# The attention's value products on one core: feature-major float32 for all query blocks, two kv heads in the two halves of a bank

## The chip, the cores and the metric

The kernel runs on one core of a Trainium2 chip. The metric is the device time of one execution in microseconds (us). The engines that matter here are TensorE (PE in the profile; its weight loads stand apart as PEld), VectorE (DVE), ScalarE (ACT), GpSimd (POOL) and SyncE (SP, which issues most DMAs). They run side by side, each through its own instructions in order, and wait for one another by semaphores.

## The reference, cut to what matters

```
def dsa_mixer(x, cos, sin, w_in, w_o):          # 512 tokens, 16 heads of 64, 4 kv heads, top_k = 128
    q, k, v, iq, ik, iw = split(x @ w_in)       # q, k, iq, ik get partial rotary
    for each block of 128 queries:
        score  = sum over index heads of iw * relu(iq . ik / 8), causal
        sel    = top_k(score, 128)
        logits = q . k[sel] / 8, -inf where not causal       # each kv head serves 4 heads
        p      = softmax(logits)
        o      = p @ v[sel]
    return o @ w_o
```

The whole is four sub-layers: this attention, a squared-ReLU MLP, a gated linear attention (GLA), another MLP, each followed by a layer norm. float32 in and out.

## The kernel before, in words

Products are made in one of two ways. `float32r` operands are streamed once; where accuracy needs it an operand is split into a high and a low float32r part (`split`, `stack_q`, `stack_k`, the pairs `hi, lo`), and two or three products are summed. `float32` operands are multiplied as they are; the trace shows two TensorE records for each such matmul, one for other dtypes and for transposes.

The attention works on 16 steps, `steps[i] = (b, g)`: query block b of 128 queries (0 to 3), kv head g (0 to 3) with its four heads. Block b sees (b + 1) key blocks kb of 128 keys. Selection is a mask: `top_k` finds the 128 best scores of each row and leaves -1e30 on the others in `sc[b]`.

- `logits(i, j)` makes the scores of head j of step i into a `qk` bank (two of them), VectorE adds the mask and takes the row's extreme (`pr`, `mx`, L704), ScalarE takes the exponential in place (L708, or L710, which also sums the row into `den`).
- `turn(i, kb)` transposes the four heads' 128 x 128 probabilities into a `tps` bank (L717), and ScalarE copies them to a tile `pT` of 128 keys x 512 (four heads of 128 queries): L720 for blocks 0 and 1; L725 for blocks 2 and 3, where VectorE also takes the low part (L726).
- `values(i)`, for blocks 0 and 1 (`b < STACKED`): token-major float32. For each head and kb the probabilities are the weights and `vn[:, kb, g, :]` is streamed, 64 values and a column of ones (65 columns), into the `po` bank; the ones give the softmax's denominator (L735, 48 matmuls). VectorE divides (L747, L738).
- `values_t(i, kb)`, for blocks 2 and 3: feature-major float32r. The weights are v's high and low parts side by side (`vs`, 128 columns, made once by `split_v`), 512 columns of probabilities are streamed, high and then low (L768, L769, 28 each). `back` then copies the sum to SBUF (L774), transposes it back (L779), and adds the two halves and divides (L781, L782, L783), once for each step.
- After a block's four steps `to_xt` transposes the block's output for the output projection.

`blocks` writes the steps so that the logits of step i + 1 stand between the turns of step i. The values of blocks 2 and 3 follow their turns by `LAG`. The projections of the remaining queries (`natural`, L197 to L199) and of the output (`out_first`) are written between the steps.

The order that runs is not that of the source: a scheduler sets each engine's order as the kernel is built, and takes ready matmuls of a projection in between. The pools bound it: three `ps` banks (projections, and the feature-major sums), two `qk`, one `po`, two `tps`, eight `pT` tiles.

One other place in the kernel bears on this: in the GLA, L990 and L997 are float32 matmuls whose outputs lie in 64 or 32 of a bank's 128 partitions, for L997 in four neighbouring strips of 32, one after the other.

Of the kernel before, what the change touches and what calls it, by code (L numbers as in the profile page):

```python
# [57 lines left out]
RAW_BUFS = 4  # L58
ORDER = (1, 2, 3, 0)
WARM_UP = (4, 6)  # L60
STACKED = 2
LAG = 3

_CF = {}

# [40 lines left out]
class Trunk:  # L106
# [504 lines left out]
    def attention(self, x, xs):  # L611

        nc, tc = self.nc, self.tc
        with tc.tile_pool(name="att", bufs=1) as ap:
            qT = [self.big.tile([P, A_H, P], F32R, name="big") for _ in range(NT)]
            kT = ap.tile([P, A_KV, 2, SEQ], F32R, name="kT")
            vn = ap.tile([P, NT, A_KV, 65], F32, name="vn")
            nc.vector.memset(vn[:, :, :, 64:65], 1.0)
            sc = [None] + [ap.tile([P, (b + 1) * P], F32, name=f"sc{b}") for b in range(1, NT)]
            with tc.tile_pool(name="idx", bufs=1) as ip, tc.tile_pool(name="ir", bufs=2) as it, \  # L620
                    tc.tile_pool(name="idt", bufs=3) as self.rt:
# [67 lines left out]
            def logits(i, j):  # L689

                b, g = steps[i]
                W = (b + 1) * P
                mb = self.cbias if b == 0 else sc[b]
                if j == 0:
                    pr = pp.tile([P, 4, 512], F32, name="pr")
                    mx = self.small.tile([P, 4], F32, name="mx")
                    den = self.small.tile([P, 4], F32, name="den") if b >= STACKED else None
                    live[i] = pr, mx, den
# [3 lines left out]
                nc.tensor.matmul(ps[:, :W], qT[b][:, h, :], kT[:, g, 0, :W], start=True, stop=False)  # L702
                nc.tensor.matmul(ps[:, :W], qT[b][:, h, :], kT[:, g, 1, :W], start=False, stop=True)
                nc.vector.tensor_tensor_reduce(out=pr[:, j, :W], in0=ps[:, :W], in1=mb[:, :W],  # L704
                                               scale=-(A_D ** -0.5), scalar=3.0e38, op0=OP.add, op1=OP.min,
                                               accum_out=mx[:, j:j + 1])
                if den is None:
                    nc.scalar.activation(pr[:, j, :W], pr[:, j, :W], AF.Exp, bias=mx[:, j:j + 1], scale=-1.0)  # L708
                else:
                    nc.scalar.activation(pr[:, j, :W], pr[:, j, :W], AF.Exp, bias=mx[:, j:j + 1], scale=-1.0,  # L710
                                         accum_out=den[:, j:j + 1])

            def turn(i, kb):

                tps = self.tp.tile([P, 4, P], F32, name="tps")
                for j in range(4):
                    nc.tensor.transpose(tps[:, j, :], live[i][0][:, j, kb * P:(kb + 1) * P], self.ident)  # L717
                if steps[i][0] < STACKED:
                    pT = ptp.tile([P, 4, P], F32, name="pT")
                    nc.scalar.copy(pT, tps)  # L720
                    live[i, kb] = pT
                else:
                    ph = ptp.tile([P, 4, P], F32R, name="pT")
                    pl = ptp.tile([P, 4, P], F32R, name="pT")
                    nc.scalar.copy(ph, tps)  # L725
                    nc.vector.tensor_sub(pl, tps, ph.bitcast(F32))  # L726
                    live[i, kb] = ph, pl

            def values(i):
                b, g = steps[i]  # L730
                po = self.po.tile([P, 512], F32, name="po")
                po = po[:, :260].rearrange("p (j d) -> p j d", d=65)
                for j in range(4):
                    for kb in range(b + 1):
                        nc.tensor.matmul(po[:, j, :], live[i, kb][:, j, :], vn[:, kb, g, :],  # L735
                                         start=kb == 0, stop=kb == b)
                on, rc = normalizer(b, g, po[:, :, 64])
                nc.vector.tensor_tensor(on, po[:, :, 0:64], rc, op=OP.mult)  # L738
                if g == A_KV - 1:
                    self.to_xt(live["on"], b)  # L740

            def normalizer(b, g, den):

                if g == 0:
                    live["on"] = op_.tile([P, DM], F32, name="on")
                rc = self.small.tile([P, 4], F32, name="rc")
                nc.vector.reciprocal(rc, den)  # L747
                on = live["on"][:, g * 256:(g + 1) * 256].rearrange("p (j d) -> p j d", d=64)
                return on, rc[:, :, None].to_broadcast([P, 4, 64])

            def split_v():

                vs = self.big.tile([P, NT * A_KV, 2, 64], F32R, name="big")
                vf = vn[:, :, :, 0:64].rearrange("p t g d -> p (t g) d")
                nc.scalar.copy(vs[:, :, 0, :], vf)
                nc.vector.tensor_sub(vs[:, :, 1, :], vf, vs[:, :, 0, :].bitcast(F32))
                live["vs"] = vs

            def values_t(i, kb):
# [8 lines left out]
                nc.tensor.matmul(ps, vs, ph, start=kb == 0, stop=False)  # L768
                nc.tensor.matmul(ps, vs, pl, start=False, stop=kb == b)  # L769
                for f in live.pop("back", []):  # L770
                    f()
                if kb == b:
# [3 lines left out]
                    def back():  # L776
                        po = self.po.tile([P, 512], F32, name="po").rearrange("p (j d) -> p j d", d=P)
                        for j in range(4):
                            nc.tensor.transpose(po[:, j, :], oT[:, j, :], self.ident)  # L779
                        on, rc = normalizer(b, g, live[i][2])  # L780
                        nc.scalar.copy(on, po[:, :, 64:128])  # L781
                        nc.vector.tensor_add(on, on, po[:, :, 0:64])  # L782
                        nc.vector.tensor_tensor(on, on, rc, op=OP.mult)  # L783
                        if g == A_KV - 1:
                            self.to_xt(live["on"], b)

# [2 lines left out]
            def blocks():  # L789

                for j in range(4):
                    logits(0, j)
                turned = []
                for i, (b, g) in enumerate(steps):
                    if (b, g) == (STACKED, 0):
                        split_v()
# [12 lines left out]
                for a in turned:  # L809
                    values_t(*a)  # L810
                for f in live.pop("back"):
                    f()

# [423 lines left out]
```

## Time and profile before

| what | value |
|---|---|
| device time, median of 3 runs | 1145.86 us (1145.68 to 1147.49) |
| the profiled execution | 1145.4 us, its span 1143.6 us |
| PE busy over the span | 1126.0 us (98%) |
| DVE busy | 883.2 us (77%) |
| ACT busy | 563.7 us (49%) |
| TensorE clock granted | 0.998 |
| blocks 0 and 1, with the projections among them | about 108 to 147 us of the span |
| block 2 | about 147 to 176 us |
| block 3, with the output projections among its steps | about 176 to 216 us |

Busy time of PE is not work at its peak: matmuls are pipelined, each record contains the way through the array, and the ends are modelled. The cost of a matmul in a stream is read from the distance of two starts. In a row of the timeline that joins n records, that is (length of the row minus length of one record) / (n - 1). Rows of groups give busy time and the mean duration of one, and the idle time of the engine just ahead of them.

### The profile page before, as it was taken

The page shows a single profiled execution, that of the slowest core. Times are in us where ns is not written, and L with a number is a line of the kernel's source. Part 1 is how long each engine was busy: PE and PEld are TensorE (multiplying, and loading weights), DVE is VectorE, ACT ScalarE, POOL GpSimd, SP SyncE. Part 2 cuts the span into 40 slices and gives each one's busy share as a digit, 9 for nine tenths or more (in the row PEclk, how much of TensorE's full clock was granted, in tenths as well). Part 3 has the DMA queues.
Part 4 walks back from the last instruction along what each step waited for, and adds up shares of the span by engine and source line. Part 5 has one row for each costly group of instructions (what it writes and reads, how often), then busy time and mean ns, then how long its engine had stood idle before and what let it go on. Part 6 is the DMA issues. An engine that isn't in the chain of part 4 may idle for free. (4 is left out here: it accounts for less than half of the span.)

```text
span 1143.6 us, 16057 instructions
## 1 busy us (share of the span) xinstructions
PE 1126.0 (98%) x6039; PEld 943.5 (82%) x6039; DVE 883.2 (77%) x1592; ACT 563.7 (49%) x973; POOL 212.9 (19%) x136
## 2 busy tenths in 40 slices
PE   9999999999999999999999999999999999999997
PEld 7887888888888888888797887888988888888875
DVE  7899997687976786786885387567696876786787
ACT  6655786543544444353356476435344444343342
POOL 0000000002123213203301255110042123213221
PEclk9999999999999999999999999999999999999999
DMA  7322130521421431441432232052222421431321
GB/s 252 98 74 75 37 112 1 154 88 38 147 84 64 148 112 47 137 142 55 112 109 77 63 112 90 23 148 74 83 91 86 148 92 56 147 117 52 127 74 74
DMA packets 58198, 109.12 MB, mean 95 GB/s; under 512 B 5205, under 2 KB 10841, under 8 KB 58121
## 3 DMA queue, kind: packets, MB, share of 16 engines
q1 hardware_dynamic: 56968, 103.91, 28.7%
q0 software_dynamic: 1152, 4.19, 1.3%
q8 instruction: 47, 0.77, 0.3%
q14 instruction: 31, 0.25, 0.1%
HBM read 105.99 MB, written 2.10 MB: 95 GB/s over the span
## 5 line engine op out<-in xcount | busy, mean ns | idle before, releaser
L142 DVE TENSOR_TENSOR w_lo<-raw,w_hi 128x1024 fp32r<-128x1024 f32 (+4 forms) x220 | 288.9, 1331 | 29.1 <-ACT w_hi L141 26.7
L141 ACT CAST w_hi<-raw 128x1024 fp32r<-128x1024 f32 (+4 forms) x220 | 223.6, 1024 | 120.6 <-PE ps L199 45.8
L197 PE MATMUL ps<-XT,w_hi 128*128 128x512 f32 (+1 forms) x640 | 236.0, 369 | 0.0
L198 PE MATMUL ps<-XT,w_hi 128*128 128x512 f32 (+1 forms) x640 | 235.5, 368 | 0.0
L199 PE MATMUL ps<-XT,w_lo 128*128 128x512 f32 (+1 forms) x640 | 235.5, 368 | 0.0
L197 PE MATMUL ps<-w_hi,XT 128*128 128x512 f32 (+5 forms) x440 | 163.7, 372 | 0.8 <-ACT w_hi L141 0.8
L198 PE MATMUL ps<-w_lo,XT 128*128 128x512 f32 (+5 forms) x440 | 160.9, 366 | 0.6 <-DVE w_lo L142 0.6
L199 PE MATMUL ps<-w_hi,XT 128*128 128x512 f32 (+5 forms) x440 | 160.3, 365 | 0.0
L198 PEld LDWEIGHTS ps<-XT,w_hi 128*128 128x128 f32 x640 | 120.7, 189 | 20.2 <-issue 0.4
L197 PEld LDWEIGHTS ps<-XT,w_hi 128*128 128x128 f32 x640 | 120.6, 189 | 20.2 <-issue 0.2
L199 PEld LDWEIGHTS ps<-XT,w_lo 128*128 128x128 f32 x640 | 120.6, 188 | 20.1 <-issue 0.2
L163 POOL TENSOR_TENSOR raw<-raw 128x1024 f32<-128x1024 f32 x14 | 34.2, 2441 | 385.4 <-DVE w_lo L142 385.4
L197 PE MATMUL ps<-w_hi,form 128*128 128x512 f32 x260 | 102.2, 393 | 0.7 <-DVE big L419 0.7
L198 PE MATMUL ps<-w_lo,form 128*128 128x512 f32 x260 | 101.4, 390 | 0.0
L199 PE MATMUL ps<-w_hi,form 128*128 128x512 f32 x260 | 101.4, 390 | 0.0
L197 PEld LDWEIGHTS ps<-w_hi,XT 128*128 128x128 f32 x440 | 82.8, 188 | 12.0 <-ACT w_hi L141 1.0
L198 PEld LDWEIGHTS ps<-w_lo,XT 128*128 128x128 f32 x440 | 82.8, 188 | 11.1 <-DVE w_lo L142 1.0
L199 PEld LDWEIGHTS ps<-w_hi,XT 128*128 128x128 f32 x440 | 82.8, 188 | 10.9
L142 DVE TENSOR_TENSOR w_lo<-t,w_hi 128x1024 fp32r<-128x1024 f32 x14 | 30.3, 2164 | 72.7 <-ACT w_hi L141 72.7
L371 DVE TENSOR_TENSOR h<-h 128x512 f32<-128x512 f32 (+1 forms) x72 | 43.7, 624 | 44.2 <-ACT h L370 44.2
L370 ACT ACTIVATE h<-ps 128x512 f32<-128x512 f32 (+1 forms) x72 | 38.7, 546 | 61.5 <-PE ps L199 54.5
L141 ACT CAST w_hi<-t 128x1024 fp32r<-128x1024 f32 x14 | 14.7, 1049 | 105.3 <-POOL t L165 105.3
(248 smaller groups left out, 1950.4 us busy)
## 6 DMA issues: line engine op xcount, KB each, us to landing
raw<-in_mlp_w_up_dram SPq DMA_DIRECT2D x64, 512.0 KB, 4.4
raw<-in_mlp_w_down_dram SPq DMA_DIRECT2D x64, 512.0 KB, 4.4
raw<-in_b_w_in_dram SPq DMA_DIRECT2D x16, 512.0 KB, 4.9
raw<-in_a_w_in_dram SPq DMA_DIRECT2D x12, 512.0 KB, 4.6
big<-in_x_dram SPq DMA_DIRECT2D x8, 512.0 KB, 4.0
raw<-in_a_w_o_dram SPq DMA_DIRECT2D x8, 512.0 KB, 4.0
raw<-in_b_w_o_dram SPq DMA_DIRECT2D x8, 512.0 KB, 4.7
raw<-in_b_w_in_dram SPq DMA_DIRECT2D x8, 346.0 KB, 3.9
```

What stands on the lines that cost most here:

```text
L141: self.nc.scalar.copy(hi, src)
L142: self.nc.vector.tensor_sub(lo, src, hi.bitcast(F32))
L163: sub(t1, b12, b11)
L197: mmul(out, lhs[0], rhs[0], start=first, stop=False, skip_group_check=more)
L198: mmul(out, lhs[0], rhs[1], start=False, stop=False, skip_group_check=more)
L199: mmul(out, lhs[1], rhs[0], start=False, stop=last, skip_group_check=more)
L370: nc.scalar.activation(h, ps[:, :step], AF.Relu)
L371: nc.vector.tensor_mul(h, h, h)
```

## The change

All four blocks now go one way, feature-major in plain float32. `turn` makes one float32 `pT` tile, with no low part. `values(i, kb)` is called for odd g only and takes the steps i - 1 and i together: two float32 matmuls of 512 columns, whose weights are v of one kv head (64 columns), the first into partitions 0 to 63 of a `ps` bank, the second into 64 to 127. `back` runs once for each pair of kv heads: four transposes bring both heads home at once, one VectorE instruction divides 512 columns by `den`. The denominators come from the exponential's row sum in all blocks. The column of ones is no longer set, `split_v` and `vs` are gone, and LAG counts positions and not turned tiles. In the lines of the changed kernel the projections are L196 to L198, the logits L701 and L702, the turns L713, the values L726, the way back L737, `to_xt` L241.

```
-STACKED = 2
-LAG = 3
+LAG = 2
...
-            nc.vector.memset(vn[:, :, :, 64:65], 1.0)
...
-                if den is None:
-                    nc.scalar.activation(pr[:, j, :W], pr[:, j, :W], AF.Exp, bias=mx[:, j:j + 1], scale=-1.0)
-                else:
-                    nc.scalar.activation(..., accum_out=den[:, j:j + 1])
+                nc.scalar.activation(..., accum_out=den[:, j:j + 1])
...
-                if steps[i][0] < STACKED:
-                    pT = ptp.tile([P, 4, P], F32, name="pT")
-                    nc.scalar.copy(pT, tps)
-                    live[i, kb] = pT
-                else:
-                    ph = ptp.tile([P, 4, P], F32R, name="pT")
-                    pl = ptp.tile([P, 4, P], F32R, name="pT")
-                    nc.scalar.copy(ph, tps)
-                    nc.vector.tensor_sub(pl, tps, ph.bitcast(F32))
-                    live[i, kb] = ph, pl
+                live[i, kb] = ptp.tile([P, 4, P], F32, name="pT")
+                nc.scalar.copy(live[i, kb], tps)
...
-                ph, pl = (a.rearrange("p j q -> p (j q)") for a in live.pop((i, kb)))
-                vs = live["vs"][:, kb * A_KV + g]
-                vs = vs.rearrange("p two d -> p (two d)")
-                nc.tensor.matmul(ps, vs, ph, start=kb == 0, stop=False)
-                nc.tensor.matmul(ps, vs, pl, start=False, stop=kb == b)
+                for m in range(2):
+                    p = live.pop((i - 1 + m, kb)).rearrange("p j q -> p (j q)")
+                    nc.tensor.matmul(ps[m * 64:(m + 1) * 64, :], vn[:, kb, g - 1 + m, 0:64], p,
+                                     start=kb == 0, stop=kb == b)
...
-                        on, rc = normalizer(b, g, live[i][2])
-                        nc.scalar.copy(on, po[:, :, 64:128])
-                        nc.vector.tensor_add(on, on, po[:, :, 0:64])
-                        nc.vector.tensor_tensor(on, on, rc, op=OP.mult)
+                        rc = self.small.tile([P, 2, 4], F32, name="rc")
+                        nc.vector.reciprocal(rc, live.pop(("den", b, g // 2)))
+                        on = live["on"][:, (g - 1) * 256:(g + 1) * 256].rearrange("p (m j d) -> p j m d", m=2, d=64)
+                        nc.vector.tensor_tensor(on, po.rearrange("p j (m d) -> p j m d", m=2), ..., op=OP.mult)
...
                         if x <= b:
                             turn(i, x)
-                            if b >= STACKED:
-                                turned.append((i, x))
-                        if len(turned) > LAG:
-                            values_t(*turned.pop(0))
-                    if i > 0 and steps[i - 1][0] < STACKED:
-                        values(i - 1)
+                            if g % 2:
+                                turned.append((now, i, x))
+                        now += 1
+                        while turned and turned[0][0] < now - LAG:
+                            values(*turned.pop(0)[1:])
```

The scheduler's order of the changed program has the 40 value matmuls in 26 runs between other TensorE work: 16 runs of one matmul, 9 of two, and one of six. Blocks 0 and 1 have 8 runs of one and 2 of two; blocks 2 and 3 the rest.

TensorE, end of block 1, before: the token-major values (L735) between logits (L702, L703), turns (L717) and the transposes of `to_xt` (L242).

```order
L702 MATMUL qk<-kT,big 128x256
L703 MATMUL qk<-kT,big 128x256
L242 MATMUL tps<-cft,on 128x128 x2
L735 MATMUL po<-vn,pT 128x65 x2
L702 MATMUL qk<-kT,big 128x256
L703 MATMUL qk<-kT,big 128x256
L735 MATMUL po<-vn,pT 128x65 x6
```

The same place now:

```order
L713 MATMUL tps<-cft,pr 128x128 x2
L726 MATMUL ps<-pT,vn 64x512
L241 MATMUL tps<-cft,on 128x128 x4
L726 MATMUL ps<-pT,vn 64x512
L241 MATMUL tps<-cft,on 128x128 x4
L726 MATMUL ps<-pT,vn 64x512
L701 MATMUL qk<-kT,big 128x256
```

The two halves of a bank no longer stand next to each other here: transposes over all 128 partitions have come in between.

TensorE in block 3, before, a turn and its two value matmuls:

```order
L702 MATMUL qk<-kT,big 128x512
L703 MATMUL qk<-kT,big 128x512
L717 MATMUL tps<-cft,pr 128x128 x4
L768 MATMUL ps<-pT,big 128x512
L769 MATMUL ps<-pT,big 128x512
```

The same place now:

```order
L713 MATMUL tps<-cft,pr 128x128 x4
L726 MATMUL ps<-pT,vn 64x512 x2
L701 MATMUL qk<-kT,big 128x512
L702 MATMUL qk<-kT,big 128x512
L713 MATMUL tps<-cft,pr 128x128 x4
```

Here the two halves have stayed together, in a run of two.

TensorE at the first turns of block 0, before: matmuls of the third query projection (L197 to L199) stand between the logits.

```order
L197 MATMUL ps<-w_hi,XT 128x512
L198 MATMUL ps<-w_lo,XT 128x512
L702 MATMUL qk<-kT,big 128x128
L717 MATMUL tps<-cft,pr 128x128
L703 MATMUL qk<-kT,big 128x128
```

The same place now:

```order
L701 MATMUL qk<-kT,big 128x128
L713 MATMUL tps<-cft,pr 128x128
L702 MATMUL qk<-kT,big 128x128
L701 MATMUL qk<-kT,big 128x128
L702 MATMUL qk<-kT,big 128x128
L713 MATMUL tps<-cft,pr 128x128 x3
```

The projection's matmuls have left block 0's logits; they now begin at block 1's first logits and stand mostly behind them.

More of the change, by code (lines that the diff above doesn't have):

```diff
@@ L696, in logits @@
                     mx = self.small.tile([P, 4], F32, name="mx")
-                    den = self.small.tile([P, 4], F32, name="den") if b >= STACKED else None
-                    live[i] = pr, mx, den
+                    if g % 2 == 0:
+                        live["den", b, g // 2] = self.small.tile([P, 2, 4], F32, name="den")
+                    live[i] = pr, mx, live["den", b, g // 2][:, g % 2, :]
                 pr, mx, den = live[i]
@@ L717, in turn, with values @@
                     nc.tensor.transpose(tps[:, j, :], live[i][0][:, j, kb * P:(kb + 1) * P], self.ident)
-                if steps[i][0] < STACKED:
-                    pT = ptp.tile([P, 4, P], F32, name="pT")
-                    nc.scalar.copy(pT, tps)
-                    live[i, kb] = pT
-                else:
-                    ph = ptp.tile([P, 4, P], F32R, name="pT")
-                    pl = ptp.tile([P, 4, P], F32R, name="pT")
-                    nc.scalar.copy(ph, tps)
-                    nc.vector.tensor_sub(pl, tps, ph.bitcast(F32))
-                    live[i, kb] = ph, pl
[L729 to L759, printed above, removed]
+                live[i, kb] = ptp.tile([P, 4, P], F32, name="pT")
+                nc.scalar.copy(live[i, kb], tps)
+            def values(i, kb):
                 b, g = steps[i]
@@ L779, in back @@
                             nc.tensor.transpose(po[:, j, :], oT[:, j, :], self.ident)
-                        on, rc = normalizer(b, g, live[i][2])
-                        nc.scalar.copy(on, po[:, :, 64:128])
-                        nc.vector.tensor_add(on, on, po[:, :, 0:64])
-                        nc.vector.tensor_tensor(on, on, rc, op=OP.mult)
+                        if g == 1:
+                            live["on"] = op_.tile([P, DM], F32, name="on")
+                        rc = self.small.tile([P, 2, 4], F32, name="rc")
+                        nc.vector.reciprocal(rc, live.pop(("den", b, g // 2)))
+                        on = live["on"][:, (g - 1) * 256:(g + 1) * 256].rearrange("p (m j d) -> p j m d", m=2, d=64)
+                        nc.vector.tensor_tensor(on, po.rearrange("p j (m d) -> p j m d", m=2),
+                                                rc.rearrange("p m j -> p j m")[:, :, :, None].to_broadcast([P, 4, 2, 64]),
+                                                op=OP.mult)
                         if g == A_KV - 1:
@@ L793, in blocks @@
                 turned = []
+                now = 0
                 for i, (b, g) in enumerate(steps):
-                    if (b, g) == (STACKED, 0):
-                        split_v()
                     for x in range(4):
@@ L801, in blocks @@
                             turn(i, x)
[L802 to L807 removed]
+                            if g % 2:
[3 more added lines that the diff above has]
+                            values(*turned.pop(0)[1:])
                     yield
[L809 to L810 removed]
+                for _, i, x in turned:
+                    values(i, x)
                 for f in live.pop("back"):
```

4 lines of the change are left out of this document (2 added, 2 removed).

## The prediction

> **What bounds the kernel now.** I read the page's busy times first, then the stages of the attention by windows, then who waits there, then the groups of instructions, and last the timeline for the distance of starts. The page:
>
> ```profile
> PE 1126.0 (98%) x6039; PEld 943.5 (82%) x6039; DVE 883.2 (77%) x1592; ACT 563.7 (49%) x973; POOL 212.9 (19%) x136
> ```
>
> The windows of blocks 0 and 1, block 2, block 3 (columns: length, then busy us of each engine, the granted clock and DMA):
>
> ```profile
> 108.00:147.00 39.00, 37.99 (x265) 32.72 (x263) 36.36 (x131) 30.88 (x64) 0.00 (x0) 1.00 0.14 43
> 147.00:176.00 29.00, 28.55 (x189) 24.30 (x188) 27.56 (x79) 26.60 (x72) 0.00 (x0) 1.00 0.27 90
> 176.00:216.00 40.00, 40.00 (x220) 32.79 (x219) 25.12 (x63) 23.54 (x55) 2.27 (x4) 1.00 0.12 37
> ```
>
> TensorE has work nearly all the time, at full clock, and DMA is light. DVE is also close to full in the first window, DVE and ACT in the second; in the third TensorE stands alone. So the change is priced on TensorE, and the other engines count where they make it wait. Its waits, first in 105 to 147, then in 147 to 216:
>
> ```profile
> PEld qk L702 <- DVE mx L704: 2.3, 5, 0.8
> ...
> PEld tps L717 <- DVE pT L726: 0.8, 3, 0.3
> PEld tps L717 <- DVE XT L245: 0.6, 1, 0.6
> ...
> PEld ps L769 <- DVE pT L726: 0.2, 1, 0.2
> ```
>
> Only 1.0 us of waiting on the low part (L726) is there to win back, although that group is 19.3 us of DVE. What follows the attention is bound by TensorE as well (98%), so a difference here is carried to the end.
>
> **Prices on TensorE.** The timeline:
>
> ```profile
> 118.62 1.05 PE L735 MATMUL po<-vn,pT 128*128 128x65 f32 x8
> ...
> 645.65 0.32 PE L198 MATMUL ps<-w_lo,XT 128*128 128x346 f32 x1
> 645.81 0.32 PE L199 MATMUL ps<-w_hi,XT 128*128 128x346 f32 x1
> 646.06 0.55 PE L997 MATMUL qk<-Q,gk 128*32 128x48 f32 x32
> 646.54 0.42 PE L197 MATMUL ps<-w_hi,XT 128*128 128x346 f32 x1
> 646.80 0.32 PE L198 MATMUL ps<-w_lo,XT 128*128 128x346 f32 x1
> 646.96 0.32 PE L199 MATMUL ps<-w_hi,XT 128*128 128x346 f32 x1
> ...
> 663.79 0.31 PE L199 MATMUL ps<-w_hi,XT 128*128 128x346 f32 x1
> 664.03 0.68 PE L990 MATMUL qk<-E 128*64 128x64 f32 x8
> ...
> 700.05 0.39 PE L197 MATMUL ps<-w_hi,XT 128*128 128x512 f32 x1
> 700.28 0.39 PE L198 MATMUL ps<-w_lo,XT 128*128 128x512 f32 x1
> ...
> 716.42 1.02 PE L1051 MATMUL po<-big,AT 128*128 128x256 f32 x4
> 717.28 1.03 PE L1051 MATMUL qk<-big,AT 128*128 128x256 f32 x4
> ...
> 719.00 0.60 PE L1034 MATMUL tps<-cft,E 128*128 128x128 f32 x4
> ```
>
> And the groups (busy us, mean ns, idle before):
>
> ```profile
> L726 DVE TENSOR_TENSOR pT<-tps,pT 128x512 fp32r<-128x512 f32 x28 | 19.3, 689 | 3.7 <-ACT pT L725 2.8
> L768 PE MATMUL ps<-pT,big 128*128 128x512 f32 x28 | 12.4, 442 | 0.0
> L735 PE MATMUL po<-vn,pT 128*128 128x65 f32 x96 | 12.4, 268 | 0.0
> L769 PE MATMUL ps<-pT,big 128*128 128x512 f32 x28 | 11.9, 423 | 0.0
> L710 ACT ACTIVATION_READ_ACCUMULATOR pr<-pr,mx 128x1 f32 x32 | 6.4, 200 | 0.0
> L779 PE MATMUL po<-cft,pT 128*128 128x128 f32 x32 | 4.8, 274 | 0.0
> L774 ACT COPY pT<-ps 128x512 f32<-128x512 f32 x8 | 4.8, 600 | 0.9 <-PE ps L769 0.9
> L783 DVE TENSOR_TENSOR on<-on,rc 128x256 f32<-128x256 f32 x8 | 3.4, 423 | 0.2
> L782 DVE TENSOR_TENSOR on<-on,po 128x256 f32<-128x256 f32 x8 | 3.3, 416 | 0.2
> L738 DVE TENSOR_TENSOR on<-po,rc 128x256 f32<-128x256 f32 x8 | 3.3, 416 | 0.0
> L781 ACT COPY on<-po 128x256 f32<-128x256 f32 x8 | 3.0, 379 | 0.7 <-PE po L779 0.6
> ```
>
> - A float32r matmul of 512 columns: 700.28 - 700.05 = 0.23 us.
> - Float32, 65 columns: (1.05 - 0.27) / 7 = 0.11 a record, two records, 0.22 us.
> - Float32, 256 columns: 717.28 - 716.42 = 0.86 for four records, so 0.43 a matmul. 512 columns then take 0.86 us, 3.7 times float32r. The number of weight columns does not shorten it: L990, 64 columns of weights and 64 streamed, needs (0.68 - 0.22) / 7 = 0.066 a record, against 0.054 by columns.
> - Side by side: L997 is 16 float32 matmuls of 48 columns in four strips. One after another they would need 16 x 0.43 x 48 / 256 = 1.29 us. From first start to last start are 0.55 - 0.21 = 0.34, with the last stream 0.38: 3.4 at a time. L990's four lie in one strip and do not overlap. So neighbours in different strips overlap, and I take a pair in two halves at 0.86 for both. A pair with an instruction over all 128 partitions in between can't, since the order on the engine holds: 0.86 each.
> - Going into strips and out: from L199 at 645.81 to L198 at 646.80 are 0.99 us. The two projections around are worth 0.16 each (645.65 to 645.81, 646.80 to 646.96), the strips 0.38. That leaves 0.29 us for one excursion: late start of the first, late start of the next, whose successor is late too. Float32 as such isn't the cause: L1051 to L1034 and the projections around them follow without a gap of this size. Bounds: 0.20 if only the two late starts count (646.06 - 645.97 and 646.54 - 646.44), 0.32 with reading error.
>
> In the Trainium skill, TensorEngine Tiling (Array Packing), Key Properties, a change of the tiling mode drains TensorE, while a change of tile within a mode does not. The page has no price for it; were there no such drain, the sum below would lose its excursions and come to +0.6 us, and with the row's 0.29 it is +8.1. The trace agrees with the rule.
>
> **The sum, part by part.**
> 1. Removed: 48 x 0.22 = 10.6 (blocks 0, 1) and 56 x 0.23 = 12.9 (blocks 2, 3), 23.5 us of TensorE.
> 2. Added: 40 matmuls in 26 runs. 16 runs of one and 9 of two take 0.86 each, the one of six takes three times that: 28 x 0.86 = 24.1. Streamed whole and always paired it would be 20 x 0.86 = 17.2; the scheduler's order costs 6.9 of it.
> 3. Excursions: 26 x 0.29 = 7.5 (5.2 to 8.3).
> 4. The transposes home: 32 before (8 steps), 32 now (8 pairs), at (0.60 - 0.27) / 3 = 0.11. Nothing; 1.7 us move from blocks 2 and 3 to blocks 0 and 1.
>
> TensorE: 24.1 + 7.5 - 23.5 = +8.1. By stage: blocks 0 and 1 +2.7 (10 x 0.86 + 10 x 0.29 + 1.7 - 10.6), blocks 2 and 3 +5.5.
>
> 5. DVE in blocks 2 and 3 loses 19.3 (L726) and 3.3 (L782), and one division of 512 columns replaces two of 256. TensorE wins the 1.0 us of its waits on L726; at most the waits of that window on DVE together, about 2.
> 6. Lost cover: in block 0 the logits wait for DVE (the 2.3 us above), and the projection's nine matmuls between them (9 x 0.23 = 2.1) have moved behind. They covered waits; DVE's own work there hardly changes (two divisions less, top-k as before). Between 0 and 2.1, taken as 1.0.
> 7. ACT in blocks 0 and 1 gets 32 row sums (6.4) and four copies of a sum (2.4), and loses one copy of v (1.0): 30.9 + 7.8 = 38.7 of 39 us. On the way from exponential to turn 0.2 us more each. I cost this at nothing since TensorE's own +2.7 lengthens that window and gives ACT room to 41.7; if that cover fails it is the third rival.
> 8. The feature-major sums of blocks 0 and 1 now take `ps` banks, which the projections use. Three are there, and the projections mostly stand behind; nothing, or one wait of a stream (0.9). The removed memset and v's split (one each, under 1.3 us of DVE) are hidden by TensorE.
>
> Sum: 8.1 - 1.0 + 1.0 = +8.1 us against the profiled execution's own 1145.4 us (span 1143.6 and 1.8 around it, 0.5 below the median of the runs). Forecast 1153.5 us, 0.7% slower.
>
> **Rivals.**
> - Excursions are hidden (other side: faster). The 0.29 was seen around short streams of 48 columns; a stream of 0.86 us may give time to load the next weights and to change over. Then +0.6 remains on TensorE, and DVE's relief of up to 2.2 decides: 1143.8 us. The point from which it decides: an excursion under 0.06 us. Against it: the first late start comes before the strips stream at all (0.09 at L997; at L990 the projection ahead starts at 663.79 and lasts 0.16, so 0.08 too), and no length of theirs can hide it; 26 x 0.09 is 2.3 us. 0.07; half hidden would be 1149, in my range.
> - Halves do not overlap: only strips of 32 were seen. Then 12 pairs more at 0.86, +10.3: 1163.8 us. For it only that 64-wide neighbours don't occur in this trace. 0.07.
> - ACT sets the pace of blocks 0 and 1. The highest share the trace shows over a stage is 26.60 of 29 (92%); at that share 38.7 us need 42.1, 3.1 over the window, about what TensorE adds there anyway (2.7). If the waits of both add up and do not overlap, 8.1 + 3.1: 1156.6 us. 0.14.
> - The relief is larger: TensorE's records hide waits, and all waiting of block 2 goes (28.55 of 29 busy, yet by the prices above about 2 us of it is not streaming). Together with excursions at 0.20: 8.1 - 2.3 - 2.2 - 1.0 = +2.6, 1148.0. 0.10, half of it below the bound of what can be told.
>
> **How the numbers follow.** The main case has 0.62: 1153.5, from 1149.0 (short excursions, full relief, no lost cover) to 1159.6 (dear excursions, lost cover 2.1, a bank wait, some ACT). A measurement of this kernel tells 0.2%, 2.3 us, from no change. Faster than that: the larger part of the first rival, 0.06. Within: its rest and half of the fourth, 0.07. Slower: the rest, 0.87. The range reaches down towards the fourth rival and up over ACT's: 1147.8 to 1160.5, which leaves out the first rival and the second, and a little of the main case.
>
> **What would show it.** L726 (the new value matmuls) as 80 records of 64 weight columns, first and second half with starts a few ns apart in runs of two, 0.86 us and more apart where broken; 0.3 us between the neighbours of a run beyond its stream; no subtraction into `pT` on DVE, whose busy time falls by some 23 us; TensorE still over 95% busy from 108 us to the attention's end, which comes about 8 us later. The forecast is wrong if starts of the halves lie 0.43 us or more apart in runs of two, if the excursion is far from 0.29, or if TensorE's waits on ACT in blocks 0 and 1 grow beyond 3 us.

## The result, and the profile after

The changed kernel takes 1159.33 us (median; 1157.71 to 1160.01), the kernel before 1145.80 us beside it. The ratio is 1.0109, with a 95% interval from 1.0094 to 1.0123: 13.5 us slower. Forecast were 1153.5 us, within 1147.8 to 1160.5.

The profiled execution took 1157.71 us with a span of 1155.9, against 1143.6 before: 12.3 us. The first line of the page:

```profile
PE 1136.3 (98%) x5967; PEld 931.2 (81%) x5967; DVE 861.7 (75%) x1538; ACT 564.3 (49%) x996; POOL 212.8 (18%) x136
```

DVE has lost 21.5 us and TensorE has gained 10.3, at the same share. Where the time lies is read from marks, the starts of some instructions in both traces:

| mark | before, us | after, us | difference |
|---|---|---|---|
| first logits of block 0 (128 columns) | 108.44 | 108.31 | -0.1 |
| first logits of block 1 (256 columns) | 119.49 | 121.57 | +2.1 |
| first logits of block 2 (384 columns) | 145.01 | 150.29 | +5.3 |
| first logits of block 3 (512 columns) | 165.00 | 171.49 | +6.5 |
| first ReLU of the MLP | 252.62 | 263.31 | +10.7 |
| end | 1143.63 | 1155.94 | +12.3 |

So 5.3 us come in blocks 0 and 1, 5.4 in blocks 2 and 3 with what follows them, and 1.6 far behind the attention, where no line was changed. Windows of the changed kernel over blocks 0 and 1, over block 2, and over block 3 (length, busy us of PE, PEld, DVE, ACT, POOL, then TensorE's clock, DMA share and GB/s):

```profile
108.00:147.00 39.00, 35.76 (x189) 25.22 (x188) 35.05 (x116) 29.96 (x85) 0.00 (x0) 0.96 0.23 70
147.00:180.00 33.00, 33.00 (x176) 19.86 (x176) 17.79 (x58) 27.25 (x72) 0.00 (x0) 1.00 0.12 46
180.00:228.00 48.00, 47.87 (x238) 32.36 (x237) 16.19 (x46) 25.36 (x55) 2.28 (x4) 1.00 0.09 21
```

In the first window TensorE has fallen from 37.99 to 35.76 of 39 us, and its clock is 0.96 where it was 1.00. From 147 us on it is full as before, and DVE, nearly full in block 2 before (27.56 of 29), is at 17.79 of 33. The waits between 105 and 147 us show who holds TensorE up:

```profile
PEld qk L701 <- DVE mx L703: 2.6, 4, 1.0
...
PE qk L701 <- DVE mx L703: 2.0, 4, 0.9
PEld ps L726 <- ACT pT L715: 1.9, 4, 0.8
PEld tps L713 <- ACT pT L715: 1.3, 2, 0.8
```

The logits' matmuls themselves now wait 2.0 us for DVE, with nothing between them. Before, from 105 to 216 us, these were all the waits of matmuls that the view lists:

```profile
PE qk L702 <- DVE mx L704: 0.6, 2, 0.4
PE tps L717 <- DVE XT L245: 0.3, 1, 0.3
```

So 0.6 us of the 2.3 were waits of matmuls, and the rest was a wait of weight loads with matmuls still in the pipe. Block 0 in three windows, and the same stretch of the kernel before in two:

```profile
108.00:114.00 6.00, 3.94 (x27) 3.00 (x26) 5.97 (x26) 5.94 (x17) 0.00 (x0) 0.99 0.00 1
114.00:117.40 3.40, 3.40 (x14) 2.26 (x14) 3.28 (x15) 2.83 (x13) 0.00 (x0) 0.51 0.00 0
117.40:121.50 4.10, 3.74 (x20) 1.99 (x17) 3.06 (x14) 2.83 (x10) 0.00 (x0) 1.00 0.00 0
```

```profile
108.00:114.00 6.00, 5.22 (x35) 3.80 (x34) 5.96 (x26) 5.70 (x12) 0.00 (x0) 1.00 0.00 1
114.00:119.50 5.50, 5.42 (x42) 4.62 (x41) 5.50 (x29) 4.17 (x12) 0.00 (x0) 1.00 0.00 0
```

TensorE is busy for 3.94 of the first 6 us instead of 5.22, and then its clock stands at half speed for 3.4 us. The trace of the kernel before has half clock only at its end.

The new value matmuls, as a group and on the timeline (start, duration of the row, then the operation; each matmul is two records):

```profile
L726 PE MATMUL ps<-pT,vn 128*64 128x512 f32 x80 | 30.7, 629 | 0.7 <-ACT pT L715 0.7
```

```profile
154.55 0.45 PE L701 MATMUL qk<-kT,big 128*128 128x384 f32 x1
154.83 0.34 PE L702 MATMUL qk<-kT,big 128*128 128x384 f32 x1
155.10 1.08 PE L726 MATMUL ps<-pT,vn 128*64 128x512 f32 x4
156.11 0.88 PE L584 MATMUL tps<-ident_r,hl 128*128 128x128 f32 x8
...
160.78 1.07 PE L726 MATMUL ps<-pT,vn 128*64 128x512 f32 x2
161.79 0.55 PE L713 MATMUL tps<-cft,pr 128*128 128x128 f32 x3
...
219.24 2.79 PE L726 MATMUL ps<-pT,vn 128*64 128x512 f32 x12
221.96 0.66 PE L241 MATMUL tps<-cft,on 128*128 128x128 f32 x4
```

Two matmuls side by side (x4) take 1.01 us from their start to the next instruction's, one alone (x2) also 1.01: the halves overlap fully, their records start 6 to 7 ns apart, and a broken pair pays twice. Six matmuls take 2.72, so a stream is (2.72 - 1.01) / 2 = 0.86 us. What is over in a run of one, 0.15, with the late start of the first record (0.09) and of the instruction behind the next (0.06 to 0.11), makes 0.30 to 0.36 for an excursion (a change into strips and out again) in all runs where nothing was waited for.

### The profile page after: what moved, and what is told of

Read it like the earlier page. It is cut to its first block, busy times and chain, and to the rows that moved or that the text cites. A ratio compares the mean times of both kernels' runs of the same rounds, so it can differ in the third digit from the quotient of the medians.

```text
span 1155.9 us, 15873 instructions
## 1 busy us (share of the span) xinstructions
PE 1136.3 (98%) x5967; PEld 931.2 (81%) x5967; DVE 861.7 (75%) x1538; ACT 564.3 (49%) x996; POOL 212.8 (18%) x136
## 3 DMA queue, kind: packets, MB, share of 16 engines
q1 hardware_dynamic: 56968, 103.91, 28.4%
## 5 line engine op out<-in xcount | busy, mean ns | idle before, releaser
L196 PE MATMUL ps<-XT,w_hi 128*128 128x512 f32 (+1 forms) x640 | 236.0, 369 | 0.0
L197 PE MATMUL ps<-XT,w_hi 128*128 128x512 f32 (+1 forms) x640 | 235.5, 368 | 0.0
L198 PE MATMUL ps<-XT,w_lo 128*128 128x512 f32 (+1 forms) x640 | 235.5, 368 | 0.0
L196 PE MATMUL ps<-w_hi,XT 128*128 128x512 f32 (+5 forms) x440 | 164.2, 373 | 0.8 <-ACT w_hi L140 0.8
L197 PE MATMUL ps<-w_lo,XT 128*128 128x512 f32 (+5 forms) x440 | 161.3, 367 | 0.6 <-DVE w_lo L141 0.6
L198 PE MATMUL ps<-w_hi,XT 128*128 128x512 f32 (+5 forms) x440 | 160.8, 366 | 0.0
L196 PEld LDWEIGHTS ps<-XT,w_hi 128*128 128x128 f32 x640 | 120.7, 189 | 20.3 <-issue 0.2
L197 PEld LDWEIGHTS ps<-XT,w_hi 128*128 128x128 f32 x640 | 120.7, 189 | 20.2 <-issue 0.4
L198 PEld LDWEIGHTS ps<-XT,w_lo 128*128 128x128 f32 x640 | 120.7, 189 | 20.1 <-issue 0.2
L196 PE MATMUL ps<-w_hi,form 128*128 128x512 f32 x260 | 102.2, 393 | 0.7 <-DVE big L418 0.7
L197 PE MATMUL ps<-w_lo,form 128*128 128x512 f32 x260 | 101.4, 390 | 0.0
L198 PE MATMUL ps<-w_hi,form 128*128 128x512 f32 x260 | 101.3, 390 | 0.0
L196 PEld LDWEIGHTS ps<-w_hi,XT 128*128 128x128 f32 x440 | 83.0, 189 | 13.0 <-ACT w_hi L140 1.0
L197 PEld LDWEIGHTS ps<-w_lo,XT 128*128 128x128 f32 x440 | 83.2, 189 | 11.5 <-DVE w_lo L141 1.0
L198 PEld LDWEIGHTS ps<-w_hi,XT 128*128 128x128 f32 x440 | 83.2, 189 | 11.2
```

The costliest lines, as they stand in the source:

```text
L196: mmul(out, lhs[0], rhs[0], start=first, stop=False, skip_group_check=more)
L197: mmul(out, lhs[0], rhs[1], start=False, stop=False, skip_group_check=more)
L198: mmul(out, lhs[1], rhs[0], start=False, stop=last, skip_group_check=more)
```

## Experiments

All numbers in one table. The marks are of the one profiled execution and stand against the kernel before. Where the clock was at half at 24 us, 2.1 to 2.4 us of every mark in that row come from there. The last column says where TensorE's clock stood at half speed for 3.41 us, or for twice that (x2), in that execution (the end of the span, after the last matmuls, left out).

| kernel | median, us | ratio to before, 95% | block 2's first logits | first ReLU | end | half clock at, us |
|---|---|---|---|---|---|---|
| changed | 1159.33 | 1.0109 (1.0094 to 1.0123) | +5.3 | +10.7 | +12.3 | 114, 694 |
| paired | 1152.65 | 1.0053 (1.0040 to 1.0066) | +4.0 | +5.3 | +6.9 | 112 x2, 689 |
| padded | 1160.43 | 1.0120 (1.0106 to 1.0134) | +5.3 | +14.3 | +14.2 | 111 x2 |
| all0 | 1153.72 | 1.0058 (1.0045 to 1.0070) | +5.0 | +4.9 | +6.4 | 114 x2, 687 |
| all0banks | 1148.42 | 1.0017 (1.0008 to 1.0027) | -0.8 | +0.9 | +2.4 | 684 |
| tail | 1149.77 | 1.0018 (1.0008 to 1.0027) | -0.1 | +1.8 | +3.3 | 686 |
| mixed | 1148.80 | 1.0006 (0.9997 to 1.0015) | -0.9 | +1.5 | +3.0 | 684 |
| half01 | 1154.47 | 1.0066 (1.0050 to 1.0082) | +5.7 | +6.8 | +6.8 | 111 x2 |
| half01b | 1149.00 | 1.0017 (1.0008 to 1.0025) | +1.8 | +4.1 | +4.0 | 24 |
| half23 | 1155.45 | 1.0071 (1.0056 to 1.0086) | +2.6 | +9.6 | +11.2 | 24, 693 |
| nosum_paired | 1152.05 | 1.0041 (1.0028 to 1.0055) | +5.0 | +6.3 | +7.9 | 24, 113 x2, 690 |
| tiny_strip | 1175.35 | 1.0252 (1.0237 to 1.0267) | | | | 24, 700 |
| tiny_full | 1159.01 | 1.0113 (1.0097 to 1.0129) | | | | none |

**Pairs kept together (paired).**

```diff
-                nc.scalar.copy(live[i, kb], tps)
+                live["copy", i, kb] = nc.scalar.copy(live[i, kb], tps)
...
+                    tc.add_manual_dep(mm.ins, live["copy", i, kb].ins.name, ...)
```

> The changed kernel, with one dependency more: the first half's value matmul of a key block also waits for the copy of the second half's turned probabilities, so that the scheduler leaves nothing between the two. The 40 matmuls then stand in 18 runs (two of one, fourteen of two, one of four, one of six) with 21 streams one after another, against 26 runs and 28 streams in the changed kernel. Theory (the loss is on TensorE: a broken pair streams twice, and each change into strips and out costs 0.30 us): 7 x 0.86 + 8 x 0.30 = 8.4 us less, from 1159.3 to about 1151. Rival, ACT sets the pace of blocks 0 and 1: only what is saved in blocks 2 and 3 shows, 3 x 0.86 + 4 x 0.30 = 3.8, about 1155.5. Rival, excursions cost nothing and only streams count: 6.0 less, 1153.3. Rival, halves that stand side by side do not overlap: only the 2.4 of the excursions, 1157.

1152.65 us, 6.4 us below the changed kernel by the ratios. By time alone this lies between the theory and "only streams count". The marks say more: up to the first ReLU 5.4 us are won although the half clock in block 0 lasted 3.4 us longer, and 4.1 of them come behind block 2's first logits, where 3.8 were expected (3 x 0.86 + 4 x 0.30). In blocks 0 and 1 only 1.3 of the expected 4.6 appear. One more window at half clock there is part of what is missing; the rest is also what the rival, ACT as the pace, would give, and nosum_paired below prices that at about 1 us.

**No strips at all (padded).**

```diff
-            vn = ap.tile([P, NT, A_KV, 65], F32, name="vn")
+            vn = ap.tile([P, NT, 2, 3, 64], F32, name="vn")
+            nc.gpsimd.memset(vn[:, :, :, 1, :], 0.0)
...
+                    w = vn[:, kb, g // 2, m:m + 2, :].rearrange("p s d -> p (s d)")
+                    nc.tensor.matmul(ps, w, p, start=kb == 0 and m == 0, stop=kb == b and m == 1)
```

> The changed kernel without strips: v stands with 64 columns of zeros beside each head, so that each of the 40 value matmuls has 128 columns of weights and adds both heads into the whole bank (zeros to the other half); one pT buffer less. The same order, no halves side by side and no change of strips. Theory: 40 x 0.86 = 34.4 us for the values instead of 28 x 0.86 + 26 x 0.30 = 31.9, so 2.5 slower than the changed kernel, about 1161.8. Rival, the change into strips and out costs nothing: 34.4 against 24.1, 10.3 slower, about 1169.6. Rival, the halves never overlap and the excursions cost 0.30: 34.4 against 42.2, 7.8 faster, about 1151.5.

1160.43 us, 1.3 us above the changed kernel by the ratios, where 2.5 were expected and 10.3 if excursions cost nothing. Without strips 12 streams more cost about what 26 excursions cost. Both rivals are far off, so the overlap of halves and the price of the excursions are both real, and nearly cancel in the order of the changed kernel.

**The excursion by itself (tiny_strip, tiny_full).** Added to the kernel before, behind each k of the MLP's second half, once into a strip and once whole:

```diff
+            if tiny is not None:
+                po = tiny
+                self.nc.tensor.matmul(po[0:64, 0:64], self.ident[:, 0:64], self.ident[:, 0:64], start=True, stop=True)
```

```diff
+                self.nc.tensor.matmul(po[:, 0:64], self.ident, self.ident[:, 0:64], start=True, stop=True)
```

> The kernel before, with 64 float32 matmuls more whose results nobody reads: one behind each of the 64 groups of three 512-column projection matmuls of the MLP's second half, 64 columns of the identity as weights into 64 partitions, 64 columns streamed. Each is a change into a strip and out again around a short stream. Theory (an excursion costs 0.30 to 0.36 us, as the trace of the changed kernel shows it): 64 x (0.11 for the stream + 0.30 to 0.36) = 26 to 30 us more, about 1175 against 1147. Rival, the excursion is hidden by the neighbours: 64 x 0.11 to 0.14 = 7 to 9 us more, the same as with full-width weights.

> The same as the kernel with 64 short float32 matmuls into strips, but with all 128 columns of the identity as weights into 128 partitions, so no change of strips; 64 columns streamed as there. Theory: 64 x 0.22 or less (two records of at least 0.11, as the 65-column matmuls of the kernel before) = 7 to 14 us more; the difference to the strips, 64 x 0.2 to 0.3 = 13 to 19 us, is the price of the excursions alone. Rival, float32 among float32r is what costs: the same time as the strips, some 28 us more.

28.4 and 12.1 us more, both as expected. The timeline, first of the strip, then of the whole (one round of three projection matmuls and the small one):

```profile
230.86 0.33 PE L222 MATMUL po<-cft 128*64 128x64 f32 x2
231.12 0.50 PE L197 MATMUL ps<-w_hi,XT 128*128 128x512 f32 x1
231.46 0.39 PE L198 MATMUL ps<-w_lo,XT 128*128 128x512 f32 x1
231.69 0.40 PE L199 MATMUL ps<-w_hi,XT 128*128 128x512 f32 x1
232.01 0.33 PE L222 MATMUL po<-cft 128*64 128x64 f32 x2
```

```profile
228.34 0.33 PE L222 MATMUL po<-cft 128*128 128x64 f32 x2
228.48 0.47 PE L197 MATMUL ps<-w_hi,XT 128*128 128x512 f32 x1
228.79 0.39 PE L198 MATMUL ps<-w_lo,XT 128*128 128x512 f32 x1
229.02 0.40 PE L199 MATMUL ps<-w_hi,XT 128*128 128x512 f32 x1
229.26 0.33 PE L222 MATMUL po<-cft 128*128 128x64 f32 x2
```

A round takes 1.15 us with the strip and 0.92 without: 0.23 for the change into the strip and out, (28.4 - 12.1) / 64 = 0.25 by the times. The strip starts 0.32 us behind the last projection, the whole matmul 0.24; the next projection starts 0.26 us behind the strip, 0.14 behind the whole matmul; the projections hide neither. Float32 among float32r, the rival, costs 12.1 / 64 = 0.19 per matmul, no more than its own stream (two records of 0.11 at most).

**One half of the blocks (half23, half01).** The old way is kept in blocks 0 and 1 (half23, the edit below), or in blocks 2 and 3 (half01, made from the kernel before).

```diff
-                            if g % 2:
+                            if b >= STACKED and g % 2:
```

> The new way in blocks 2 and 3 alone; blocks 0 and 1 token-major in float32, as before. 28 new matmuls in 16 runs with 19 streams one after another. Theory (TensorE's prices): 19 x 0.86 + 16 x 0.30 - 56 x 0.23 - 1.7 (16 transposes home fewer) = 6.6, less 1.0 that DVE no longer holds up: 5.6 us more than before, 1152.6 against 1147.0. Rival, the loss is made in block 0 where the cover is lost: within 1.5 us of the kernel before.

> The new way in blocks 0 and 1 alone; blocks 2 and 3 feature-major in float32r, as before. 12 new matmuls in 10 runs with 10 streams one after another. Theory by TensorE's prices: 10 x 0.86 + 10 x 0.30 + 1.7 - 10.6 = 2.7 us more; with the lost cover in block 0 and a half-clock window there 1 to 4 more on top: 3.7 to 6.7 us, 1150.7 to 1153.7 against 1147.0. Rival, only the prices count and what was lost in block 0 is hidden by the projections: 2.7 us or less, 1149.7. Rival, ACT (now with row sums and sums to copy in blocks 0 and 1) is what holds TensorE up there: also above 3.7, but then TensorE's waits on ACT in these blocks exceed 3 us and its waits on DVE stay as before.

Each half costs: 1155.45 and 1154.47 us. In half23's profile 7.2 us lie behind the start of the attention (9.6, less 2.4 that the half clock at 24 us had cost before), 1.6 above the theory; the rival that all is lost in block 0 falls. In half01's, 6.8 lie in the attention with two half-clock windows in block 0. Both times are above what was expected. The sum of the two, 15.7 by the ratios, is above the 12.5 of the changed kernel. By the marks up to the first ReLU it is 7.2 + 6.8 = 14.0 against 10.7; some 1.5 of that (an estimate) is the second half-clock window of half01, and where the rest comes from stays open.

**A pair's matmuls in one piece, and what stands in block 0 (all0, all0banks).**

```diff
-                            if g % 2:
-                                turned.append((now, i, x))
+                            if g % 2 and x == b:
+                                turned += [(now, i, kb) for kb in range(b + 1)]
```

The matmuls of a pair then also wait for the copy of its last turned probabilities, and `LAG` is 0. For the second kernel also

```diff
-                    live["o"] = self.mm.tile([P, 512], F32, name="ps")
+                    live["o"] = self.po.tile([P, 512], F32, name="po")
...
-                        po = self.po.tile([P, 512], F32, name="po").rearrange("p (j d) -> p j d", d=P)
+                        po = self.tp.tile([P, 4, P], F32, name="tps")
```

> The changed kernel with a pair's value matmuls of all key blocks together, behind the copy of the last turned probabilities: 11 runs (six of two, two of four, two of six, one of eight) with 20 streams. Theory: values cost 20 x 0.86 + 11 x 0.30 = 20.5 us instead of 31.9, so 11.4 less; up to 1.5 of it lost again in block 0, where nothing stands between the logits any more: 1148 to 1149.5. Rival, ACT sets the pace of blocks 0 and 1: what is saved in blocks 2 and 3 shows alone (some 6), about 1153. Rival, the rest of the loss is float32 streaming as such (40 matmuls whatever their order): within 1 us of the changed kernel.

> As the one with a pair's matmuls together, and the feature-major sums take a bank of po, the way back a bank of tps, in place of ps and po: the runs stay the same (11, 20 streams), but eleven matmuls of the projection stand between block 0's logits again, where nothing stood. Theory (block 0 of the changed kernel lost the work that covered waits for DVE, and with TensorE idle there its clock fell to half for 3.4 us): 1.0 to 3.7 us less than with ps, 1144.5 to 1147.5, so about the kernel before or a little faster. Rival, the fillers cover nothing since DVE sets block 0's end anyway: the same time as with ps, within 0.7 us.

The first missed: 5.8 us below the changed kernel by the ratios, not 10 to 11.4. The second, with the same runs and streams, is 4.7 us below the first, more than the 3.7 expected at most. Block 0 in both, without and with the projection between the logits:

```profile
108.00:114.00 6.00, 3.94 (x28) 2.95 (x26) 5.93 (x26) 5.69 (x16) 0.00 (x0) 0.98 0.01 1
114.00:121.00 7.00, 7.00 (x29) 5.05 (x30) 5.67 (x25) 4.67 (x18) 0.00 (x0) 0.53 0.00 0
```

```profile
108.00:114.00 6.00, 5.33 (x34) 3.89 (x34) 5.97 (x26) 5.60 (x17) 0.00 (x0) 1.00 0.00 1
114.00:121.00 7.00, 6.60 (x36) 3.89 (x36) 6.93 (x32) 5.70 (x23) 0.00 (x0) 1.00 0.00 0
```

With the fillers TensorE is busy 5.33 of the first 6 us and keeps its clock; without them it is busy 3.94 and then runs at half clock for 6.8 us. At the first ReLU the two differ by 4.0 us. Two half-clock windows at the price that they have behind the attention (1.4 to 1.6, below) would be about 3 of it, an estimate; the lost cover and the clock were not parted in a run of their own, and the price of a window inside block 0 was not measured.

What keeps all0banks from the 3 us below the kernel before that the prices give is partly seen. Where before no matmul of the attention waited for ACT, now:

```profile
PE tps L739 <- ACT pT L734: 0.7, 1, 0.7
PE po L726 <- ACT pT L715: 0.7, 1, 0.7
PE tps L713 <- ACT pT L715: 0.7, 2, 0.4
PE tps L739 <- ACT pT L715: 0.6, 2, 0.3
```

2.7 us, of which the last pair has half: its eight matmuls stand behind the last copy, and the way home behind theirs. The rest, some 1.2 us of the 3.9 between the prices (-3.0) and the mark (+0.9), stays open.

**The tail, and the better half of each (tail, mixed).** tail lets the last pair's key blocks follow their own copies; mixed takes `po` for the sums, and `tps` for the way back, in blocks 0 and 1 alone.

```diff
+                            if i == len(steps) - 1:
+                                turned.append((now, i, x))
```

```diff
+                    live["o"] = self.po.tile(...) if b < 2 else self.mm.tile(...)
...
```

> As the kernel with a pair's matmuls together and sums in po, but the last pair's key blocks follow their own copies, so that its eight matmuls do not all stand behind the last copy. 13 runs, 20 streams. In the kernel with the last pair together TensorE waited 0.8 us ahead of its last run and 0.8 behind it (entry 0.89 and exit 1.34 us, where 0.09 and 0.53 are usual). Theory: 1.6 us of waits less, two excursions more (0.7), and two streams ahead of the end of the turns: 1 to 2 us less, 1146.5 to 1147.5, about the kernel before. Rival, the waits only move with the last copies: the same 1148.4.

> A pair's matmuls together in all blocks; sums in po and the way back in tps in blocks 0 and 1 alone, sums in ps and the way back in po in blocks 2 and 3. The same 11 runs and 20 streams as with the one or the other throughout. Measured so far, against the kernel before: up to the first 384-column logits -0.8 us with po and +5.0 with ps; from there to the first ReLU of the MLP +1.7 with po and -0.1 with ps. Theory (block 0 wants the projection between its logits, which po gives; blocks 2 and 3 want the way back off the banks of the turns): both good halves, -0.9 us, 1146.2 against 1147.1, hardly to be told from no change. Rival, what po loses in blocks 2 and 3 is projection work moved out of blocks 0 and 1 and not its banks: as with po throughout, 1148.4 to 1149.

The tail came out as its rival: 1.0018 against 1.0017, and in its trace the last run still starts 0.8 us late. mixed is 1.0006 (0.9997 to 1.0015), by its ratio not to be told from the kernel before, and the best version of the new way. Executions with the same granted clock are closer to like with like, and there it is a little slower: at 0.998 mixed took 1146.9 to 1147.2 us and the kernel before 1145.2 to 1146.3; at 0.996 to 0.997, 1148.5 to 1149.4 and 1146.8 to 1147.7. Its mark at the first ReLU, +1.5, agrees. The good half that was expected in blocks 2 and 3 did not come (+2.4 us there, not -0.1), so the differences that marks show between two stages are in part work that has only moved, as the rival had it.

**The new way in blocks 0 and 1 alone, mended (half01b).** half01 with the edits of all0banks.

> The new way in blocks 0 and 1 alone, with a pair's matmuls together, sums in po and the way back in tps; blocks 2 and 3 as before. 12 new matmuls in 5 runs with 6 streams, and block 0's logits have the projection between them again. Theory: 6 x 0.86 + 5 x 0.33 + 1.7 - 10.6 = -2.1 on TensorE, of which waits for the way back's copies may take 1 to 2: 1145 to 1147, against 1154.5 for the same blocks with broken pairs and lost cover, and 1147.0 for the kernel before. Rival, block 0 and 1 lose by the added work of ACT whatever the order: 1150 or more.

1149.0 us, ratio 1.0017: 5.5 us below half01, so most of what half01 lost was order and cover, and not the way itself. The hoped-for gain of up to 2 us over the kernel before is absent. DVE is busy for 41.05 of the 42 us around these blocks:

```profile
107.00:149.00 42.00, 39.93 (x229) 28.67 (x228) 41.05 (x134) 34.36 (x97) 0.00 (x0) 1.00 0.10 31
```

**ACT's row sums (nosum_paired).**

```diff
+                if b < 2:
+                    nc.scalar.activation(pr[:, j, :W], pr[:, j, :W], AF.Exp, bias=mx[:, j:j + 1], scale=-1.0)
```

The row sums of blocks 0 and 1, and with them the division, are left out.

> The kernel with paired halves, without the 32 row sums on ACT in blocks 0 and 1 (their divisor is set to one by POOL, so these two blocks come out undivided); the same 18 runs. ACT loses 32 x 0.20 = 6.4 us of its work in a stage of 39. Theory (TensorE and the cover in block 0 set the pace, ACT does not): at most 0.7 us less than with the sums, 1152 against 1152.65. Rival (ACT sets the pace of blocks 0 and 1): 3 us less, 1149.5.

1152.05 us, 0.6 below paired; by the ratios 1.4 with intervals that overlap. That is nearer to the theory (0.7 at most) than to the 3 us of the rival: ACT has a share, about 1 us. The marks agree: from block 0's first logits to the first ReLU nosum_paired takes 0.9 us less than paired. The first window of blocks 0 and 1, paired and then without the sums:

```profile
108.00:147.00 39.00, 35.87 (x198) 26.74 (x197) 36.22 (x119) 30.51 (x86) 0.00 (x0) 0.91 0.25 81
```

```profile
108.00:147.00 39.00, 36.47 (x202) 27.88 (x200) 36.71 (x116) 27.36 (x56) 0.00 (x0) 0.91 0.22 69
```

ACT has 3.15 us less to do in it and TensorE hardly does more: the stage waits for something else.

## Why the prediction was right, and where it was not

Slower was right, and so was the main reason: TensorE, by broken pairs and excursions. The size was 5.8 us short by the medians, 4.2 by the profiled executions (12.3 against 8.1): 1.6 in blocks 0 and 1, 0.9 in blocks 2 and 3, and 1.6 behind them. By parts:

- Removed (part 1), 23.5 us: a little small. Adding the distances from each matmul's start to the next one's, the 152 records of the old values took 25.0.
- Added (part 2), 28 streams of 0.86: confirmed, apart from one pair in block 0 that ran at half clock, its halves starting 0.64 us apart (2.02 us in place of 1.01); halves overlap, and padded shows that without the overlap 12 streams more are paid.
- Excursions (part 3), 26 x 0.29: 0.30 to 0.36 were measured around long streams and 0.23 to 0.25 around short ones. So 26 of them cost 0.3 to 1.8 us more than forecast; that this and the 1.5 of part 1 go opposite ways is luck. Much of it shows in the neighbours: by the distances of starts the values themselves cost 3.9 us more than the old ones, the turns 3.6, the logits 3.1, the transposes home and into XT 2.1, and the projections 1.8 less. These 10.9 are the whole change up to the first ReLU, waits and the half clock included.
- Transposes home (part 4): 32 as before.
- DVE's relief (part 5), 1.0 gained: not seen. The prediction took waits of weight loads (PEld) for waits of TensorE. Before, no matmul waited for the subtraction L726 (the two rows of waits in the section on the result), so there was nothing to win back; half23's theory took the same 1.0 off, and the run came out 1.6 above it. In blocks 2 and 3 of the changed kernel no matmul waits at all, and with what follows they cost 5.4 where 5.5 - 1.0 was forecast.
- Lost cover (part 6), 1.0 taken out of 0 to 2.1: this is the step that failed. The place was right; of the nine projection matmuls six stood between block 0's logits in the trace before and three among block 1's first ones, and all have moved out of block 0. The price left out was the clock: with TensorE busy for only two thirds of 6 us it fell to half for one window here, and for two in the profiles of paired, padded, all0, half01 and nosum_paired. Blocks 0 and 1 cost 5.3 where 2.7 + 1.0 was forecast; the 1.6 over fit one window at the price measured behind the attention, an estimate. In that window lies the run of two that took 2.02 us in place of 1.01. all0 against all0banks, 4.0 us at the first ReLU, is lost cover and clock together, with two windows.
- ACT (part 7) at nothing: nearly right; taking 6.4 us of work off it gave 0.6 us by the medians and 1.4 by the ratios, and matmuls of blocks 0 and 1 waited 1.2 us for it.
- `ps` banks (part 8) at nothing, or one wait of 0.9: wrong in its consequence, and the same mistake as the lost cover. The sums hold one of the three banks of the projections, and this moved the fillers: with the sums in `po` and the way back in `tps` eleven of them stood between the logits again, and block 0 kept its clock.
- Nothing was forecast behind the attention. 1.6 us were lost there to a half-clock window, which hangs on where a grid of windows lies and not on the change (last section). The medians widen the gap by another 1.6 us. The changed kernel's three other executions, 1158.8 to 1160.0 us, have a granted clock of 0.994 against 0.995 in the profiled one, which fits one window more (3.41 x 0.5 / 1158 = 0.0015 off the mean, an estimate); where it lay was not traced.

Of the rivals, hidden excursions and halves that do not overlap are refuted by tiny_strip and padded. ACT as the pace is about 1 us, and the larger relief did not come.

The best version tried is mixed: with 20 streams in 11 runs it comes to within 0.2% of the kernel before, but not below it. The prices alone would put it 3 us below. Per pair and key block of blocks 2 and 3 four float32r matmuls (4 x 0.23 = 0.92 us) are exchanged for one float32 stream of 0.86, so the change lives on DVE's relief alone, which the stages bound by TensorE do not need, and each excursion is a loss.

## What to carry to other kernels

Halves of the array side by side pay only if the two matmuls stand next to each other in the engine's order, and here each change into strips and out cost about as much as a third of a 512-column float32 stream (0.30 to 0.36 of 0.86 us): count runs and streams in the order, not matmuls, and tie the partners together by a dependency. Before an accumulator is given a bank of a pool, look at who else draws from it: here it was the projection that kept TensorE busy between waits, and with it gone the clock fell too. When a change leaves TensorE idle for a third of a stretch of 3 us, look at the granted clock there. The share alone does not decide (next section), but a window at half clock has a price of its own.

## What was not expected of the hardware

TensorE's clock at half speed in the middle of a full kernel. The windows last 3.413 us or a multiple, and lie on a grid: in the changed kernel's execution the one at 113.9 and the one at 694.2 us are 170 x 3.413 apart. The Trainium skill, TensorE: Matmul & The Clock Gate, Part 1, has such a window of 3413 ns that runs freely; the traces agree.

The one behind the attention comes after a wait of 2.1 us in the gated attention, which every kernel here has, the one before too:

```profile
PE qk L990 <- ACT AT L991: 2.1, 1, 2.1
```

The changed kernel around it, by windows (which lie up to 0.1 us beside the grid), first the window of the grid with the wait in it, then parts of the next:

```profile
690.87:694.28 3.41, 1.28 (x20) 1.00 (x14) 3.41 (x4) 3.38 (x6) 0.60 (x1) 0.99 0.26 39
...
694.30:697.70 3.40, 3.40 (x10) 2.68 (x9) 3.35 (x6) 0.63 (x1) 3.40 (x3) 0.51 0.98 337
697.70:702.00 4.30, 4.30 (x55) 3.36 (x54) 1.21 (x4) 2.84 (x5) 1.31 (x3) 1.00 0.53 189
```

and half01, whose grid cuts the wait in two:

```profile
684.44:687.85 3.41, 2.64 (x51) 2.29 (x49) 2.93 (x6) 2.65 (x4) 0.72 (x1) 1.00 0.00 0
687.85:691.26 3.41, 2.06 (x17) 1.75 (x18) 3.41 (x5) 2.50 (x5) 1.48 (x1) 1.00 0.49 142
```

In the nine profiles in which 1.9 us or more of the wait lay in one window of the grid, the next window ran at half clock; in the five where at most 1.6 did, the one of the kernel before among them, it did not. The price shows in how far the work behind it moved against the kernel before: 1.4 to 1.6 us with, nothing (0.1 at most) without. The Trainium skill, the same page, Why this matters for your kernels, warns of idle gaps above about 3 us; here 1.9 us sufficed, and the measurement decides.

How long TensorE is busy in a window does not decide by itself. This is block 0's window ahead of the half clock in the changed kernel:

```profile
110.59:114.00 3.41, 2.25 (x14) 1.62 (x14) 3.41 (x16) 3.36 (x14) 0.00 (x0) 0.99 0.00 0
```

TensorE is busy in it for 2.25 us of 3.41. In half01's second window above it is busy for less, 2.06 us, and full clock followed. In block 0 the six profiles without the projection between the logits have 2.05 to 2.50 us in the window ahead of the half clock, and the eight with it 2.89 or more in every window there; what else the clock goes by stays open.

Where the grid lies differs from one execution to the next, which fits the times of the kernel before. They lie in three groups, 1145.2 to 1146.3, 1146.8 to 1147.7 and 1148.9 to 1149.7 us, and the granted clock falls with them: 0.998, 0.996 to 0.997, and 0.995. By the 0.0015 of a window these are none, one and two windows at half clock ahead of the end, an estimate. A median of such times moves by 1.8 us with how many executions have a window more, so differences below 0.2% in the table are not read as causes unless executions at the same clock show them. What sets off the window at 24 us in four of the profiles (TensorE was busy throughout the 3.4 us ahead of it in each; it cost 2.1 to 2.4 us) stays open.
